# A Fourier / RG-LRU trunk on one core: the first stage emitted from a written order, its modulation vectors made as columns on TensorE, and the square roots of the last RG-LRU head split by direction

## The chip, the cores and the metric

One core of one Trainium2 chip runs the whole program. The metric is device time in microseconds (us) of one execution. Its engines are PE (TensorE matmuls; PEld is the loading of the stationary operand beside them), DVE (VectorE), ACT (ScalarE), POOL (GpSimd) and SP (SyncE), which here issues the DMAs.

## The reference, cut to what matters

128 context tokens and 1024 latent tokens, 1024 wide, pass two layers. Layer 0 mixes by a two-dimensional Fourier transform (over tokens, and over the 256 channels of each of 8 groups), layer 1 by a gated linear recurrence that runs forward and backward.

```python
def _ada(cond, w_ada, b_ada):
    m = jax.nn.silu(cond) @ w_ada + b_ada
    shift, scale, gate = jnp.split(m, 3, axis=-1)
    ...
def _layer(x, cond, p, kind, h0):
    shift, scale, gate = _ada(cond, w_ada, b_ada)
    h = _rmsnorm(x, norm_g) * (1.0 + scale) + shift
    u, z = jnp.split(h @ w_in, 2, axis=-1)
    if kind == 0:
        y = _fourier_mix(u, p["w_fmix"], p["b_fmix"])
    else:
        uc = _centred_dwconv(u, p["conv_w"], p["conv_b"])
        yf, hf = _rglru_dir(uc, ..., h0[:, 0], False)
        yb, hb = _rglru_dir(uc, ..., h0[:, 1], True)
        y = yf + yb
    out = (y * jax.nn.silu(z)) @ w_out
    return x + gate * out, state

def _rglru_dir(u, w_r, b_r, w_i, b_i, lam, h0, reverse):
    r = jax.nn.sigmoid(_blockdiag(u, w_r, b_r))
    i = jax.nn.sigmoid(_blockdiag(u, w_i, b_i))
    log_a = -LRU_C * r * jax.nn.softplus(-lam)
    bterm = jnp.sqrt(-jnp.expm1(2.0 * log_a)) * (i * u)
    ...  # h[t] = a[t] * h[t-1] + bterm[t]
```

There are two conditions, one for latent and one for context tokens, so shift, scale and gate are needed for two vectors each. Latent tokens get a position embedding first.

## The kernel before, in words

Products of fp32 operands are made of three matmuls (`mm3`, L196 to L198): each operand is split into a rounded high part (ACT copy, L185) and the rest (DVE or POOL subtraction, L186). `wload` (L190) fetches a block of weights and splits it.

**First stage (the first 109.5 us).** It folds the channel transform into `w_fmix` (`fold`, 4 blocks: 12 matmuls of 512 columns and 8 of 256 each), loads the nine token tiles x0 to x8, adds the position rows (six matmuls of one-hot rows, L315; adds at L324 on DVE and L325 on POOL) and normalises them (`xnorm`, L332 and L335, with `rsqrt_cols`, L261 to L266). A token transform follows: half differences d0 to d3 (L431) give eight PSUM tiles `psO` (12 matmuls each), quarter differences give `psT`, quarter sums `psF`. `put` (L381 on ACT, L382 on DVE) scales each result by the modulation `coef` and splits it for the next stage, whose matmuls are `pu`. The eight PSUM banks hold psO0 to psO6 and the tile `adar` at once, so psO7 starts when one of the seven has been read by `put`; `put` needs the scale.

The modulation of layer 0 is made in two ways. The scale comes from DVE: sixteen operations over 128 x 1024 (`ada_cols`, L228) multiply a block of `w_ada_0` by a row of silu values that PE has spread over all partitions (`sil`, L414). The shift comes from PE: `adar` (L445) holds 4 columns of silu stationary (`silZ`) and streams 512 columns of `w_adaN`; the row is turned into columns at the end (`adat`, L504). One row of `sil` is written to DRAM as `silD` (L463), for use in layer 1.

The order of this stage on each engine is left to the tile framework's scheduler.

**RG-LRU stage.** Here a class `Plan` (L42) lists operations with engine, cost and operands; a list scheduler orders them and they are emitted in that order (`manual_schedule`). Of each of 16 channel tiles m and two directions d, PE makes the gate products `g`, ACT makes `tr` and `ti` (L1053), `nu` (L1059) and `ga` (L1063), then `roots` (L1070) takes the square root for both directions of a tile in one operation, with a load of another activation table before and after it. DVE follows with L1074 to L1088 and the scans (L1096 forward, L1099 reverse), the sum of both (L1111) and the product with the branch `szz` (L1138), which goes to DRAM as `gD` (L1141, L1142). The list of `h` runs over 8 heads of two tiles each (14 and 15 are the last two).

**Output stage.** `out_stage` reads `gD` back by rows `gr` (L717), splits them into `gh` and `gl` (L185, L186; the first three `gl` on POOL) and makes the tiles `o` from them and `w_out` (`wo`).

Of the kernel before, what the change touches and what calls it, by code (L numbers as in the profile page):

```python
# [28 lines left out]
GAP = 3  # L29
NG = SP + GAP + S + GAP  # L30
# [12 lines left out]
class Plan:  # L43

    def __init__(self, bufs):
        self.bufs, self.ops, self.touch, self.free = bufs, [], {}, set()

    def given(self, key):
        self.free.add(key)

    def add(self, eng, cost, fn, r=(), w=(), lat=None):
        i = len(self.ops)
        if lat is None:
            lat = 0.3 if eng == "PE" else 0.12
        pre = set()
        for k in list(r) + list(w):
            pre |= {j for j, wr in self.touch.get(k, []) if wr or k in w}
        for k in list(r) + list(w):
            self.touch.setdefault(k, []).append((i, k in w))
        self.ops.append(dict(eng=eng, cost=cost, fn=fn, lat=lat, pre=pre))  # L60

    def order(self):
        ops = self.ops
        for (tag, n), us in self.touch.items():
            old = self.touch.get((tag, n - self.bufs[tag]))
            if old and us and (tag, n) not in self.free:
# [15 lines left out]

# [7 lines left out]
        assert len(topo) == n, "cycle"  # L90
# [15 lines left out]
        free, end, start = {}, {}, {}
        wait = [len(o["pre"]) for o in ops]
        ready = {i for i in range(n) if not wait[i]}
        while ready:
            best = {}  # L110
            for i in ready:
                o = ops[i]
                e = max([free.get(o["eng"], 0.0)] + [end[j] + lag(j, i) for j in o["pre"]])
                best.setdefault(o["eng"], []).append((e, i))
            pick = None
            for eng, c in best.items():
                e0 = min(c)[0]
                e, i = min((x for x in c if x[0] <= e0 + 0.15), key=lambda x: late[x[1]])
                if pick is None or e < pick[0]:
                    pick = e, i  # L120
            e, i = pick
            start[i], end[i] = e, e + ops[i]["cost"]
            free[ops[i]["eng"]] = end[i]
            ready.discard(i)
            for j in suc[i]:
                wait[j] -= 1
                if not wait[j]:
                    ready.add(j)
        self.start, self.end = start, end
# [16 lines left out]
def body(tc, nc, a):  # L146
# [76 lines left out]
    def ada_cols(layer, mts, sil, junk, tile_of=raw_tile):  # L223
        for mt in mts:
            w = tile_of(f"wada{layer}_{mt}")
# [68 lines left out]
    def xload(t):  # L294
        x = xb.tile([128, D], F32, tag="x", name=f"x{t}", bufs=8)
        SY.dma_start(x, a["x_all"][t * 128:(t + 1) * 128, :])
        return x

    posR, posC = [None] * 4, [None] * 2
    pos = xp.tile([80, 512], F32, tag="dr", name="pos", bufs=2)  # L300
    SY.dma_start(pos, a["pos"])
    hot = xb.tile([128, D], F32, tag="x", name="hot", bufs=8)

    for n, (kind, i) in enumerate((("R", 0), ("C", 0), ("R", 2), ("C", 1), ("R", 1), ("R", 3))):
        oh = hot[:, n * 128:n * 128 + 128]
        if kind == "C":
            lo, hi = 0, 64
            V.tensor_copy(oh[lo:hi].rearrange("p (r c) -> p r c", r=4),
                          ident[lo:hi, 32 * i:32 * i + 32].rearrange("p (o c) -> p o c", o=1).broadcast_to([64, 4, 32]))
        else:  # L310
            lo, hi = 64, 80
            V.tensor_copy(oh[lo:hi].rearrange("p (r c) -> p r c", r=4),
                          ident[lo:hi, 64 + 4 * i:68 + 4 * i].rearrange("p (r o) -> p r o", o=1).broadcast_to([16, 4, 32]))
        pt = ps(f"pos{kind}{i}")
        PE.matmul(pt, oh[lo:hi], pos[lo:hi], start=True, stop=True)  # L315
        if kind == "R":
            posR[i] = pt
        else:
            posC[i] = xp.tile([128, 512], F32, name=f"posC{i}")
            A.copy(posC[i], pt)  # L320

    def xpos(t, x):
        if t > 0:
            V.tensor_tensor(x[:, 0:512], x[:, 0:512], posR[(t - 1) // 2], op=ALU.add)  # L324
            PL.tensor_tensor(x[:, 512:1024], x[:, 512:1024], posC[(t - 1) % 2], op=ALU.add)  # L325

    def xnorm(ts, xs):
        for t, x in zip(ts, xs):
            ss = xb.tile([128, 1], F32, tag="ss", name=f"ss{t}", bufs=2)
            jk = xp.tile([128, D], BF16, tag="jk", name=f"jk{t}")  # L330
            xpos(t, x)
            A.activation(jk, x, AF.Square, accum_out=ss)  # L332
            rsqrt_cols(rs[:, t:t + 1], ss, xb, f"rs{t}", 1)
            if t == 0 or t > 4:
                A.activation(x, x, AF.Identity, scale=rs[:, t:t + 1])  # L335

    dh, dl = [], []

    def dft_load(j):
        n = 512 if j < 5 else 260  # L340
        r = xp.tile([128, n], F32, tag="dr", name=f"dr{j}", bufs=2)
        SY.dma_start(r, a["tdft"][j][:, 0:n])
        p = xp if j < 4 else xb
        if j < 4:
            h = p.tile([128, n], F32R, tag="dh", name=f"dh{j}", bufs=4)
            lo = p.tile([128, n], F32R, tag="dl", name=f"dl{j}", bufs=4)
        else:
            h = p.tile([128, n], F32R, name=f"dh{j}")
            lo = p.tile([128, n], F32R, name=f"dl{j}")
        A.copy(h, r)  # L350
        PL.tensor_tensor(lo, r, h.bitcast(F32), op=ALU.subtract)
        dh.append(h)
        dl.append(lo)

    def fold(gp, w):
        wh, wl = w
        wh = wh.rearrange("p (g j n) -> p g j n", g=2, j=2)
        wl = wl.rearrange("p (g j n) -> p g j n", g=2, j=2)
        gs = slice(2 * gp, 2 * gp + 2)
        for which in range(3):  # L360
            pt = ps(f"fold{gp}_{which}")
            o = pt.rearrange("p (g n) -> p g n", g=2)
            if which < 2:
                for j in range(2):
                    sl = slice(j * 128, j * 128 + 128)
                    mm3(o, fch[:, which, sl], fcl[:, which, sl], wh[:, :, j, :], wl[:, :, j, :], j == 0, j == 1)
                hl = (Ahl, Bhl)[which]
                A.copy(hl[0][:, gs, :], pt)
                V.tensor_tensor(hl[1][:, gs, :], pt, hl[0][:, gs, :].bitcast(F32), op=ALU.subtract)
            else:  # L370
                for i in range(2):
                    g = 2 * gp + i
                    for j in range(2):
                        al = alt[:, j, 8 - g:136 - g]
                        PE.matmul(o[:, i, :], al, wh[:, i, j, :], start=j == 0, stop=False)
                        PE.matmul(o[:, i, :], al, wl[:, i, j, :], start=False, stop=j == 1)
                A.copy(R[:, gs, :], pt)
                V.tensor_tensor(R[64:96, gs, :], pt[64:96, :], R[64:96, gs, :].bitcast(F32), op=ALU.subtract)

    def put(src, c, q, hi, lo):  # L380
        A.activation(hi, src, AF.Identity, scale=sc_a(0, c, q))  # L381
        V.scalar_tensor_tensor(lo, src, sc_a(0, c, q), hi.bitcast(F32), op0=ALU.mult, op1=ALU.subtract)  # L382


    silT = xb.tile([128, KD, 2], F32, name="silT")
    A.activation(silT, condT, AF.Tanh, scale=0.5)
    V.scalar_tensor_tensor(silT, silT, 1.0, condT, op0=ALU.add, op1=ALU.mult)
# [910 lines left out]
```

## Time and profile before

| | us |
|---|---|
| three runs | 1508.64, 1510.70, 1511.09 |
| median | 1510.7 |
| the profiled execution, its own time | 1507.78 |
| its span in the trace | 1506.0 |

The time of the profiled execution is taken like that of the runs; the span runs from the first to the last instruction in its trace and leaves out 1.8 us around them. All times of rows count from the span's start. Busy shares over the span: PE 97%, DVE 72%, ACT 49%, POOL 15%. An engine that is 97% busy over the whole can still idle in a stage; which stage that is has to be read from the trace by stretches.

### The profile page before, as it was taken

The page shows a single profiled execution, that of the slowest core. Times are in us where ns is not written, and L with a number is a line of the kernel's source. Part 1 is how long each engine was busy: PE and PEld are TensorE (multiplying, and loading weights), DVE is VectorE, ACT ScalarE, POOL GpSimd, SP SyncE. Part 2 cuts the span into 40 slices and gives each one's busy share as a digit, 9 for nine tenths or more (in the row PEclk, how much of TensorE's full clock was granted, in tenths as well). Part 3 has the DMA queues.
Part 4 walks back from the last instruction along what each step waited for, and adds up shares of the span by engine and source line. Part 5 has one row for each costly group of instructions (what it writes and reads, how often), then busy time and mean ns, then how long its engine had stood idle before and what let it go on. Part 6 is the DMA issues. An engine that isn't in the chain of part 4 may idle for free.

```text
span 1506.0 us, 21530 instructions
## 1 busy us (share of the span) xinstructions
PE 1462.0 (97%) x8362; PEld 1418.6 (94%) x8362; DVE 1084.6 (72%) x1588; ACT 738.6 (49%) x1110; POOL 229.1 (15%) x208
## 2 busy tenths in 40 slices
PE   8879999999999999999999999999999999899996
PEld 5458999999999999999999999999999998799996
DVE  6996445899864586747987887878787878676453
ACT  7363233322223454428756666666666666364231
POOL 6576865000001011100000000000000003000000
PEclk9979999999999999999999999999999999899998
DMA  7523667887655666621112121212121112686451
GB/s 271 184 91 108 209 200 251 307 274 238 219 192 172 198 208 221 197 86 57 48 55 72 44 72 44 72 45 72 44 63 54 58 58 84 201 284 213 147 189 48
DMA packets 81848, 212.73 MB, mean 141 GB/s; under 512 B 9345, under 2 KB 40577, under 8 KB 81617
## 3 DMA queue, kind: packets, MB, share of 16 engines
q1 hardware_dynamic: 81746, 211.36, 42.3%
q8 instruction: 65, 1.06, 0.3%
q14 instruction: 37, 0.30, 0.1%
HBM read 171.98 MB, written 39.35 MB: 140 GB/s over the span
## 4 chain that ended last, share of the span: by engine, by line
PE 48%; DVE 2%; ACT 1%; issue 1%; DMA 1%; POOL 0%; DVEq 0%; POOLq 0%; ACTq 0%
PE o L198 4%; PE o L196 4%; PE o L197 4%; PE u L198 4%; PE u L196 4%; PE u L197 4%; PE g L196 4%; PE zz L196 4%; PE zz L198 4%; PE zz L197 4%; PE g L197 4%; PE g L198 4%; DMA gr<-gD 1%; DVE nu L1099 0%; POOL gl L186 0%
## 5 line engine op out<-in xcount | busy, mean ns | idle before, releaser
L228 DVE SCALAR_TENSOR_TENSOR sil1j<-wada,sil 128x1024 bf16<-128x1024 f32 x64 | 78.0, 1219 | 10.8 <-DMA wada<-w_ada 10.6
L1016 DVE SCALAR_TENSOR_TENSOR uc<-u,tab,uc 128x1156 f32<-128x1156 f32 (+2 forms) x54 | 69.2, 1288 | 20.5 <-ACT u L999 19.1
L534 POOL TENSOR_TENSOR xr<-xr,tab 128x384 f32<-128x384 f32 (+1 forms) x24 | 23.4, 977 | 362.7 <-DMA xr<-xT 346.5
L1097 POOL COPY st<-nu 128x1 f32<-128x1 f32 x16 | 10.4, 648 | 434.0 <-DVE nu L1096 433.7
L1074 DVE SCALAR_TENSOR_TENSOR nu<-ga,nu 128x1156 f32<-128x1156 f32 x32 | 43.5, 1359 | 45.3 <-ACT tr L1070 45.3
L834 DVE SCALAR_TENSOR_TENSOR x<-o,ada,xr 128x128 f32<-128x128 f32 (+1 forms) x64 | 31.6, 513 | 58.9 <-PE o L198 56.8
L1053 ACT ACTIVATE tr<-g,gb 128x386 f32<-128x386 f32 (+1 forms) x96 | 55.4, 585 | 25.6 <-PE g L198 21.3
L185 ACT CAST gh<-gr 128x384 fp32r<-128x384 f32 x80 | 39.7, 511 | 54.9 <-DMA gr<-gD 54.7
L1002 ACT ACTIVATE uc<-u,tab 128x386 f32<-128x386 f32 (+1 forms) x48 | 32.4, 674 | 60.8 <-PE u L198 60.8
L1127 ACT ACTIVATE szz<-zz 128x386 f32<-128x386 f32 (+1 forms) x48 | 23.6, 495 | 74.7 <-PE zz L198 74.5
L186 DVE TENSOR_TENSOR gl<-gr,gh 128x384 fp32r<-128x384 f32 x77 | 40.7, 554 | 26.5 <-ACT gh L185 26.2
L625 ACT CAST uh<-pu 128x256 fp32r<-128x256 f32 (+1 forms) x32 | 12.7, 398 | 89.3 <-PE pu L198 89.1
L1053 ACT ACTIVATE ti<-g,gb 128x386 f32<-128x386 f32 (+1 forms) x96 | 52.3, 578 | 7.9 <-PE g L198 6.7
L626 DVE TENSOR_TENSOR ul<-pu,uh 128x256 fp32r<-128x256 f32 (+1 forms) x32 | 14.4, 453 | 54.9 <-ACT uh L625 54.9
L1084 DVE SCALAR_TENSOR_TENSOR ti<-ti,uc 128x1156 f32<-128x1156 f32 x32 | 42.9, 1357 | 9.6 <-ACT ti L1053 9.3
L1080 DVE SCALAR_TENSOR_TENSOR tr<-ga,tr 128x1156 f32<-128x1156 f32 x32 | 46.4, 1451 | 0.7
L741 ACT ACTIVATE sz<-z 128x384 f32<-128x384 f32 x48 | 23.1, 488 | 48.1 <-PE z L198 24.5
L1063 ACT ACTIVATE ga<-tr,sm 128x1156 f32<-128x1156 f32 x32 | 43.1, 1350 | 3.2 <-DVE nu L1099 2.0
L1059 ACT ACTIVATE nu<-tr,sp2p 128x1156 f32<-128x1156 f32 x32 | 43.4, 1356 | 1.2 <-DVE nu L1111 0.2
L1099 DVE TENSOR_TENSOR_SCAN nu<-ga,tab,ti 128x1155 f32<-128x1155 f32 x16 | 43.9, 2745 | 0.1
L1088 DVE TENSOR_TENSOR ti<-ti,tr 128x1156 f32<-128x1156 f32 x32 | 43.4, 1356 | 0.3
L1096 DVE TENSOR_TENSOR_SCAN nu<-ga,ti 128x1156 f32<-128x1156 f32 x16 | 40.9, 2555 | 0.4
(1856 smaller groups left out, 5681.0 us busy)
## 6 DMA issues: line engine op xcount, KB each, us to landing
wo<-w_out SPq DMA_DIRECT2D x96, 512.0 KB, 4.3
wada<-w_ada SPq DMA_DIRECT2D x40, 512.0 KB, 4.2
wz<-w_z SPq DMA_DIRECT2D x32, 512.0 KB, 4.0
gr<-gD SPq DMA_DIRECT2D x80, 192.0 KB, 3.6
yD<-y SPq DMA_DIRECT2D x16, 576.0 KB, 5.0
zy<-yD SPq DMA_DIRECT2D x16, 576.0 KB, 6.5
wu<-w_u SPq DMA_DIRECT2D x16, 512.0 KB, 3.8
wg<-w_gate SPq DMA_DIRECT2D x16, 512.0 KB, 3.6
```

Source lines behind the costliest of these rows:

```text
L196: PE.matmul(out, wh, xh, start=first, stop=False)
L197: PE.matmul(out, wh, xl, start=False, stop=False)
L198: PE.matmul(out, wl, xh, start=False, stop=last)
L228: V.scalar_tensor_tensor(junk, w, 0.5, sil[:, q, :], op0=ALU.mult, op1=ALU.mult, accum_out=ada[:, layer, mt, q:q + 1])
L1016: V.scalar_tensor_tensor(T["uc", m][:, lo:hi], T[ut][:, lo + t:hi + t], convw[:, m, t:t + 1], T["uc", m][:, lo:hi], op0=ALU.mult, op1=ALU.add)
L1053: A.activation(T[tg, n][:, lo:hi], T["ps", p][:, 0:hi - lo], AF.Tanh, scale=0.5, bias=gb2[:, 2 * d + mat, m:m + 1])
L1059: A.activation(T["nu", n], T["tr", n], AF.Tanh, scale=sp2[:, d, m:m + 1], bias=sp2[:, d, m:m + 1])
L1063: A.activation(T["ga", n], T["tr", n], AF.Exp, scale=sm4[:, d, m:m + 1], bias=sm4[:, d, m:m + 1])
L1074: V.scalar_tensor_tensor(T["nu", n], T["ga", n], 1.0, T["nu", n], op0=ALU.add, op1=ALU.mult)
L1080: V.scalar_tensor_tensor(T["tr", n], T["ga", n], 1.0, T["tr", n], op0=ALU.add, op1=ALU.mult)
L1088: V.tensor_tensor(ti, ti, T["tr", n], op=ALU.mult)
L1099: V.tensor_tensor_scan(nu[:, 0:L][:, ::-1], ga[:, 0:L][:, ::-1], ti[:, 0:L][:, ::-1], h0[:, 1, m:m + 1], ALU.mult, ALU.add)
```

## The change

The first stage is put in a `Plan` too, with the orders of SP and PE written out as strings (`DORD` for the DMAs; `PORD`, `QORD0`, `QORD1` for blocks of PE work), and the scheduler fills in ACT, DVE and POOL. `Plan` gets options for this: the engines whose order is fixed, pools as slots instead of rings, an operation that may run on DVE or POOL, an offset of rank (`boost`).

Scale and shift are both made as columns: each 128 x 128 block of the weights is stationary and the two columns of `silT` are the moving operand, 8 x 8 matmuls for the scale (PSUM tile `ada0`, blocks s0 to s7 of the order) and as many for the shift (`ada1`, h0 to h7). The sixteen DVE operations of layer 0, the `sil` matmuls and their copies, `adar`, `silZ` and `adat` are gone. `silD` is written from `silT` itself by two DMAs whose access runs over single elements.

```diff
+DORD = 'a p x1 c x5 t0 x2 x6 w0 t1 x8 w1 w2 t2 x3 w3 x7 s0 t3 s1 x4 s2 s3 s4 q s5 s6 s7 x0 h0 t4 t5 h1 h2 t6 h3 h4 h5 h6 h7'
+PORD = 'j0 f0 t40 f1 j1 f2 s0 f3 s1 t41 s2 u52 u42 j2 s3 j3 s4 t62 s5 t63 s6 s7 o3 o2 h0 o0 u74 o7 u64 h1 o5 o6 h2 o4 o1'
+QORD0, QORD1 = ('h3 h4', 'h5 h6 h7')
...
+    def ada_part(part, ks):
+        p = ("ps", f"ada{part}")
+        for k in ks:
+            def mms(k=k):
...
+                for m in range(KD):
+                    PE.matmul(T[p][:, 2 * m:2 * m + 2], w[:, m * 128:m * 128 + 128], silT[:, k, :],
+                              start=k == 0 and m == 0, stop=k == KD - 1 and m == KD - 1)
+            i = P.add("PE", 0.9, mms, r=[("raw" if part else "xs", f"wada{part}{k}"), ("silT", 0)], w=[p])
...
-            for k in range(4):
-                PE.matmul(pt[:, k * 128:k * 128 + 128], silT[:, 4 * i + k, q:q + 1].broadcast_to([128, 128]), ident,
-                          start=True, stop=True)
-            V.tensor_copy(sil[:, q, 512 * i:512 * i + 512], pt)
...
-                PE.matmul(pr[0:4, :], silZ[:, k, 2 - 2 * i:6 - 2 * i], w[:, 512 * i:512 * i + 512],
-                          start=k == 0 and i == 0, stop=k == KD - 1 and i == 1)
-        for k in (2 * j, 2 * j + 1):
-            ada_cols(0, [8 + k], sil, junk, lambda n: xb.tile([128, D], F32, tag="x", name=n, bufs=8))
...
-    SY.dma_start(silD, sil[0:1, :, :])
+    for q in range(2):
+        SY.dma_start(silD[0, q].rearrange("(k p) -> p k", p=128), silT[:, :, q])
```

In the list of SP the letters are a: alternating signs, p: position rows, c: channel transform, x: token tile, t: token transform, w: `w_fmix`, s and h: weights of scale and shift, q: `pdc`. POOL keeps little of the stage: most adds, the steps of the normalisation and most rests move to DVE. The first weights of the u stage are split inside the plan (`e0`, `o0`).

In the RG-LRU stage the roots of the last head are one operation for each direction, its operations get a rank offset of 30 us, and some costs of the planner change. PE's order there stays.

```diff
-            def roots():
+            def roots(ns):
                 for n in ns:
                     A.activation(T["tr", n], T["nu", n], AF.Sqrt, scale=0.25)
-            P.add("ACT", 4.9, roots, r=[("nu", n) for n in ns], w=[("tr", n) for n in ns])
+            for part in [ns] if h < 7 else [ns[0:1], ns[1:2]]:
+                P.add("ACT", 2.56 + 1.17 * len(part), lambda part=part: roots(part), r=[("nu", n) for n in part], w=[("tr", n) for n in part])
...
-                P.add("DVE", (2.56, 4.62)[d], p6, r=[("ga", n), ("ti", n)], w=[("nu", n)])
+                P.add("DVE", (2.56, 2.78)[d], p6, r=[("ga", n), ("ti", n)], w=[("nu", n)])
...
+            if h == 7:
+                P.boost = LB
```

Where the order moves, three places. The first is SP's queue at the start, before:

```order
L200 DMA tab_148<-tab 128x760
L301 DMA pos_195<-pos 80x512
L389 DMA fc_223<-fdft 128x512
L190 DMA wf0_233<-w_fmix 128x1024
L190 DMA wf1_243<-w_fmix 128x1024
L296 DMA x1_239<-x_all 128x1024
L296 DMA x5_241<-x_all 128x1024
```

and now:

```order
L239 DMA tab_148<-tab 128x760
L345 DMA dralt_212<-alt 128x272
L345 DMA drpos_219<-pos 80x512
L345 DMA x1_224<-x_all 128x1024
L721 DMA silD_117<-silT_196 128x8x1 x2
L345 DMA drfc_227<-fdft 128x512
L345 DMA x5_231<-x_all 128x1024
L345 DMA dr0_244<-tdft 128x512
L345 DMA x2_247<-x_all 128x1024
L345 DMA x6_257<-x_all 128x1024
L345 DMA wf0_273<-w_fmix 128x1024
```

The two writes of `silD` (SP waits for DVE's `silT` there) stand ahead of the channel transform and of everything else that the first fold needs, and wf0 has moved behind four token tiles.

The second is DVE at the start. Before, the rests of the first fold weights (`wf0l`, `wf1l`) come right behind the rest of the channel transform (`fcl`) and ahead of the first token tile:

```order
L396 TENSOR_TENSOR fcl_226<-fc_223,fch_225 128x512
L186 TENSOR_TENSOR wf0l_236<-wf0_233,wf0h_235 128x1024
L186 TENSOR_TENSOR wf1l_246<-wf1_243,wf1h_245 128x1024
L324 TENSOR_TENSOR x1_239<-x1_239,posR0_199 128x512
L324 TENSOR_TENSOR x5_241<-x5_241,posR2_207 128x512
```

Now the adds of x1 and x5 and their normalisation stand behind `dlfc`, and then:

```order
L465 TENSOR_TENSOR x2_247<-x2_247,posR0_229 128x512
L468 TENSOR_TENSOR x2_247<-x2_247,posC1_268 128x512
L499 SCALAR_TENSOR_TENSOR d0_282<-x1_224,rs_156,x5_231 128x1024
L465 TENSOR_TENSOR x6_257<-x6_257,posR2_240 128x512
L468 TENSOR_TENSOR x6_257<-x6_257,posC1_268 128x512
L434 TENSOR_TENSOR d1_0l_298<-d0_282,d1_0h_293 128x1024
L434 TENSOR_TENSOR wf0l_304<-wf0_273,wf0h_296 128x1024
```

The fold weights come after the first difference d0, its split and the adds of x2 and x6.

The third is ACT at tile 14, the first of the last head, before:

```order
L1063 ACTIVATE ga140_11597<-tr140_11541,sm4_6916 128x1156
L1053 ACTIVATE tr141_11607<-g14100_11581,gb2_6919 128x386
L1053 ACTIVATE tr141_11607<-g14101_11590,gb2_6919 128x384
L1053 ACTIVATE tr141_11607<-g14102_11599,gb2_6919 128x386
L1059 ACTIVATE nu141_11621<-tr141_11607,sp2p_6915 128x1156
L1063 ACTIVATE ga141_11639<-tr141_11607,sm4_6916 128x1156
L1070 ACT_TABLE_LOAD
L1070 ACTIVATE tr140_11541<-nu140_11559 128x1156
L1070 ACTIVATE tr141_11607<-nu141_11621 128x1156
L1053 ACT_TABLE_LOAD
```

and now:

```order
L1265 ACTIVATE ga140_11618<-tr140_11566,sm4_6942 128x1156
L1255 ACTIVATE tr141_11635<-g14100_11609,gb2_6945 128x386
L1272 ACT_TABLE_LOAD
L1272 ACTIVATE tr140_11566<-nu140_11590 128x1156
L1255 ACT_TABLE_LOAD
L1255 ACTIVATE tr141_11635<-g14101_11620,gb2_6945 128x384
L1255 ACTIVATE tr141_11635<-g14102_11628,gb2_6945 128x386
```

The root of direction 0 no longer waits for the gates of direction 1; the root of direction 1 follows five gate pieces, nu141, a piece of szz14 and ga141 later, with another pair of table loads.

## Rows read from the trace of the kernel before

**Rows 1.** Two lines of the page: busy time of PE, and the TensorE clock granted in 40 equal slices of the span, in tenths of full speed.

```profile
PE 1462.0 (97%) x8362; PEld 1418.6 (94%) x8362; DVE 1084.6 (72%) x1588; ACT 738.6 (49%) x1110; POOL 229.1 (15%) x208
...
PEclk9979999999999999999999999999999999899998
```

**Rows 2.** Busy time of each engine by stretches of the span; columns are the stretch, its length, PE, PEld, DVE, ACT, POOL (with instructions), the granted clock, the DMA share and GB/s.

```profile
0.00:22.30 22.30, 17.17 (x24) 6.95 (x24) 10.48 (x24) 14.37 (x25) 9.90 (x14) 1.00 0.93 353
...
71.10:94.00 22.90, 10.87 (x21) 4.69 (x21) 22.73 (x27) 9.41 (x16) 18.42 (x8) 0.63 0.37 140
94.00:109.50 15.50, 14.73 (x122) 14.38 (x120) 13.62 (x32) 12.10 (x26) 6.32 (x3) 1.00 0.34 105
...
1225.00:1272.20 47.20, 47.20 (x267) 46.89 (x265) 33.45 (x30) 35.78 (x45) 7.55 (x5) 1.00 0.19 67
1272.20:1309.00 36.80, 27.80 (x116) 24.91 (x116) 29.66 (x35) 11.79 (x21) 5.77 (x5) 0.81 0.54 171
```

**Rows 3.** What PE waited for in the first 170 us: tile and line, releaser, us in total, times, longest.

```profile
PE psO L196 <- DVE Qol L382: 7.4, 1, 7.4
PE adar L445 <- DMA wadaN<-w_adaN: 4.6, 1, 4.6
...
PE fold L375 <- DVE rs2y L264: 1.4, 1, 1.4
```

**Rows 4.** The timeline of PE in the first stage: start, us, engine, line, operation, out<-in, count and, in brackets, idle time before it. The `us` of a row overlap; the pace is the distance of the starts. Of fold block 1 the first row, and the first of block 2; of the tokens with j = 3 two rows with 15 matmuls from one to the other; the second of psO7's twelve; the first rows of psT, of psF and of the next stage.

```profile
16.22 1.22 PE L196 MATMUL fold<-wf0h,fch 128*128 128x512 f32 x2
17.24 0.63 PE L197 MATMUL fold<-wf0l,fch 128*128 128x512 f32 x1
17.66 0.63 PE L198 MATMUL fold<-wf0h,fcl 128*128 128x512 f32 x1
...
24.17 0.39 PE L196 MATMUL fold<-wf1h,fch 128*128 128x512 f32 x1
...
27.84 0.40 PE L196 MATMUL fold<-wf2h,fch 128*128 128x512 f32 x1
...
67.33 0.39 PE L198 MATMUL psO<-dh,d_3l 128*128 128x512 f32 x1
...
70.75 0.39 PE L198 MATMUL psO<-dh,d_3l 128*128 128x512 f32 x1
...
89.66 0.63 PE L197 MATMUL psO<-dl,d_0h 128*128 128x512 f32 x1
...
94.22 0.28 PE L196 MATMUL psT<-dh,d_0h 128*128 128x256 f32 x1
...
99.88 0.28 PE L196 MATMUL psF<-dh,s_0h 128*128 128x260 f32 x1
...
109.50 0.38 PE L196 MATMUL pu<-Qoh,e0h 128*128 128x256 f32 x1
```

**Rows 5.** The only fp32 matmuls of this kernel with a 128 x 128 stationary operand and two moving columns (the sums of the final normalisation): three of them, which the trace records as six, in the timeline of PE, with the matmul behind them.

```profile
524.63 0.80 PE L788 MATMUL r<-ones,ssum 128*128 128x2 f32 x6
525.30 0.42 PE L196 MATMUL o<-gh,wo0110h 128*128 128x384 f32 x1
```

**Rows 6.** Groups by line of the first 109.5 us: busy us, mean ns of one, idle time before.

```profile
L228 DVE SCALAR_TENSOR_TENSOR silj<-wada,sil 128x1024 bf16<-128x1024 f32 x16 | 30.6, 1910 | 0.3
L445 PE MATMUL adar<-wadaN,silZ 128*4 128x512 f32 x32 | 17.0, 670 | 4.6 <-DMA wadaN<-w_adaN 4.6
```

**Rows 7.** The start: timelines of SP (a DMA issue of 128 rows), ACT and DVE, in the columns of rows 4.

```profile
7.88 0.33 SPq L393 DMA_DIRECT2D altr<-alt  x1
...
3.94 0.21 ACT L386 ACTIVATE silT<-tab 128x16 f32<-128x16 f32 x1 [1.93 <-DMA tab<-tab]
...
7.82 1.04 ACT L185 CAST wf0h<-wf 128x1024 fp32r<-128x1024 f32 x1 [0.83 <-DMA wf<-w_fmix]
...
14.20 1.28 ACT L261 ACT_TABLE_LOAD   x1
...
8.90 1.22 DVE L186 TENSOR_TENSOR wf0l<-wf,wf0h 128x1024 fp32r<-128x1024 f32 x1 [1.18 <-ACT wf0h L185]
```

**Rows 8.** What PE waited for from 1240 to 1312 us and, the last row, DVE from 1225 to 1312, in the columns of rows 3.

```profile
PE o L197 <- DVE gl L186: 4.4, 3, 1.8
PE o L196 <- ACT gh L185: 2.6, 1, 2.6
...
DVE nu L1074 <- ACT tr L1070: 7.5, 2, 5.8
```

**Rows 9.** The end of the last head and the start of the output stage: timelines of ACT, DVE, SP and PE, in the columns of rows 4. The two rows of L1138 are the gated tiles 14 and 15.

```profile
1234.08 1.28 ACT L1070 ACT_TABLE_LOAD   x1
...
1236.57 1.36 DVE L1074 SCALAR_TENSOR_TENSOR nu<-ga,nu 128x1156 f32<-128x1156 f32 x1 [5.83 <-ACT tr L1070]
...
1245.07 1.35 DVE L1074 SCALAR_TENSOR_TENSOR nu<-ga,nu 128x1156 f32<-128x1156 f32 x1
...
1263.09 1.36 DVE L1138 SCALAR_TENSOR_TENSOR szz<-szz,nu 128x1155 f32<-128x1155 f32 x1
...
1299.31 1.35 DVE L1138 SCALAR_TENSOR_TENSOR szz<-szz,nu 128x1155 f32<-128x1155 f32 x1
...
1270.38 9.95 SPq L717 DMA_DIRECT2D gr<-gD  x6
...
1274.80 0.49 PE L196 MATMUL o<-gh,wo_0h 128*128 128x384 f32 x1 [2.56 <-ACT gh L185]
```

More of the change, by code (lines that the diff above doesn't have):

```diff
@@ L292, in ps, with xa @@
         return pp.tile([128, 512], F32, tag="ps", name=name)
[L294 to L297, printed above, removed]
+    P = Plan({"raw": 3, "hi": 4, "lo": 4, "xs": 4, "d": 2, "dr": 2, "dh": 4, "ps": 8}, fixed=("SP", "PE"), handles={"DVE": V, "POOL": PL})
+    T, xa_ops = {}, []
+    X = {t: ("xs" if t > 4 else "x", t) for t in range(9)}
+    def xa(i):
+        xa_ops.append(i)
+        return i
@@ L299, in body, with silu @@
+    f_raw("uL0", a["w_u0"][0][:, 0])
+    f_raw("uR0", a["w_u0"][0][:, 1])
+    silT = misc.tile([128, KD, 2], F32, name="silT")
+    def silu():
+        A.activation(silT, condT, AF.Tanh, scale=0.5)
+        V.scalar_tensor_tensor(silT, silT, 1.0, condT, op0=ALU.add, op1=ALU.mult)
+    P.add("ACT", 0.4, silu, w=[("silT", 0)])
+    hot = xp.tile([128, 768], F32, name="hot")
     posR, posC = [None] * 4, [None] * 2
-    pos = xp.tile([80, 512], F32, tag="dr", name="pos", bufs=2)
-    SY.dma_start(pos, a["pos"])
@@ L337, in body @@
[L337 to L353, printed above, removed]
@@ L359, in fold @@
+    def fold(gp):
+        ks = split_ops(("raw", f"wf{gp}"), f"wf{gp}", f"wf{gp}")
         gs = slice(2 * gp, 2 * gp + 2)
         for which in range(3):
[L361 to L372, printed above, removed]
-                    for j in range(2):
[L374 to L387, printed above, removed]
-    fc = xp.tile([128, 512], F32, tag="dr", name="fc", bufs=2).rearrange("p (w n) -> p w n", w=2)
-    SY.dma_start(fc, a["fdft"])
@@ new lines, in body, with quarter, diff, add @@
+    for key in PORD.split():
+        block(key)
+    d4 = dft_split(4)
+    def quarter(i, sub):
+        x0, x1, d = ("x", 1 + i), ("x", 3 + i), ("d", 4 + i)
+        def diff(e):
+            T[d] = xb.tile([128, D], F32, tag="d", name=f"d2_{i}", bufs=2)
+            e.tensor_tensor(T[d], T[x0], T[x1], op=ALU.subtract)
+        def add(e):
+            e.tensor_tensor(T[x0], T[x0], T[x1], op=ALU.add)
+        if sub:
+            P.add("DVE", (1.22, 2.42), diff, r=[x0, x1], w=[d])
+            return split_ops(d, f"q{i}", f"d2_{i}")
+        P.add("DVE", (1.22, 2.42), add, r=[x1], w=[x0])
+        return split_ops(x0, f"s{i}", f"s2_{i}")
```

552 lines of the change are left out of this document (358 added, 194 removed).

## The prediction

> **What bounds the kernel now.** Over the span PE is busy 97% of the time, and the granted clock dips at the left end and near the right end of the 40 slices [rows 1]. So the middle is matmul-bound at full clock, and a change to ACT, DVE or SP pays only where PE idles or runs slowly. The table of stretches shows where. From 71.1 to 94.0 us PE works 10.87 of 22.90 us at a mean granted clock of 0.63, while DVE is busy 22.73: DVE is the bound. From 1272.2 to 1309 PE works 27.80 of 36.80 us at 0.81; just before, from 1225 to 1272.2, it never idles [rows 2]. The waits name the causes. Early, psO7 waits 7.4 us for the first put (its scale comes from the sixteen DVE operations, 30.6 us in all), and adar 4.6 us for weights [rows 3, 6]. Late, `o` waits for the pieces of gD, and DVE had waited 7.5 us for the roots [rows 8]. The change touches exactly these two places, so I cost two sums.
>
> **The first stage: when does PE start, and how much has it to do?** Before, the folds start at 16.22 and the next stage at 109.50 [rows 4].
>
> The start. The six position matmuls still come first, but the fold weights now stand on ACT and DVE behind token tiles 1 and 5. Before, the table load after the first square ended at 14.20 + 1.28 = 15.5 [rows 7]; a copy of posC1 that stood ahead of it is now behind, which takes about 0.6 off. Between the load and wf0h there are then a square and a scaling of x5, a square of x2, the copy of d0 and that of wf0, five passes of about 1.04 us [rows 7], and six small operations, some 2.4 us together. That gives 22.5 for wf0h (14.9 + 5.2 + 2.4), an estimate from these rows; the rest of wf0 follows 1.22 us later. I start the folds at 22.5, **6.3 us later** than before. Bounds: 21 if ACT waits nowhere, 27 with the write of silD at its dearest (below).
>
> The work behind it, in PE's order:
> - Folds: block 1 took 27.84 - 24.17 = 3.67 us; four make 14.7. Like the first block now (0.42 us from one matmul to the next at 17.24, against 0.23 later), the first 6 us will go at half pace: +3.1 [rows 4].
> - Tokens: 15 matmuls from 67.33 to 70.75, 0.228 each; eight tiles of 12 make 21.9 [rows 4].
> - Modulation: 128 fp32 matmuls of two columns. The one like them in the trace is `r`, three in 525.30 - 524.63 = 0.67 us, 0.223 each [rows 5]; 128 take **28.5**. Lower bound: if the two records of each overlapped, 0.11 and 14.3. I take 0.223, since it is the same shape and operand type.
> - psT and psF: 14.73 busy in the stretch from 94.0 [rows 2], less 0.8 for the removed transposes of the shift row: 13.9.
>
> What goes: adar's streams (17.0 us of records that overlap, so somewhat less [rows 6]) and the waits of 7.4 and 4.6 us [rows 3]. The scale is now ready when ada0's eighth block is, ahead of psO7 and psO6 in PE's order, so their banks come free earlier. I keep 1.4 us of waiting, like that for rs2 now [rows 3]; up to 5 if the differences d2, d3 come late on DVE, whose 30.6 us of scale work [rows 6] go but which takes over adds and rests from POOL.
>
> Sum: 22.5 + 14.7 + 3.1 + 21.9 + 28.5 + 13.9 + 1.4 = **106.0**, against 109.5: a gain of 3.5. PE's work grows by more than ten microseconds; the gain is idle time, filled.
>
> **The write of silD.** SP now stands still until silT is there, about 4.4 (3.94 + 0.21 and a short DVE step), and then issues two DMAs ahead of the channel transform, x5, x2, x6 and wf0. A DMA of 128 rows holds SP 0.33 us [rows 7]; two make 0.7, which is in the sum and hidden by the position matmuls. The Trainium skill (DMA: Bandwidth & Descriptors, Rules for kernel authors) says that an access whose last dimension isn't contiguous becomes one descriptor per element, and here that is 1,024 elements in each DMA; no run shown has such a DMA. By the rows, if 1,024 elements cost like eight DMAs of 128 rows, both hold SP 16 x 0.33 = 5.3 us, 4.6 more, and all loads behind them come so much later. By that the sum would be 110.6, and the stage would be 1.1 us slower than now. I take the cheap value because the position matmuls cover a good part, and keep the other in the range.
>
> **The last head.** ACT's first root of tile 14 comes after nu141 and ga141 now; the table load stands at 1234.08 and DVE starts on it at 1236.57 after 5.83 us idle [rows 9]. With the split it follows ga140 and one gate piece directly, about 4 us earlier. The other direction can't start before its own root, and a second pair of loads (1.28 each) is in its way, so DVE's step for it stays near 1245.07 [rows 9]. Behind that the rank offset puts the head's steps next to each other: 1.36 twice, two products, two shorter ones and the scan make about 11 us, so that the gated tile 14 would be made near 1256 rather than 1263.09, and by the same count tile 15 some 10 us ahead of 1299.31.
>
> What does that give? From 1272.2 to 1309 PE does 116 matmuls; at the pace of the stretch before (47.20 / 267 = 0.177) these need 20.5 of 36.8 us, so 16.3 are lost [rows 2]. The first 2.6 go if `gr` isn't issued at 1270.38 but earlier [rows 8, 9]. The others hang on the pieces `gl`, which DVE makes between its scans (4.4 us of waiting in three [rows 8]), and on SP's queue, in which loads of `wo` and the later `gr` take turns. I take **6 of the 16.3**, between 0 (the queue hands out pieces as before) and 11 (only the clock's return and the POOL pieces remain). The two added pairs of table loads cost nothing on PE: ACT is busy 35.78 of 47.20 us there [rows 2].
>
> In the rest of the RG-LRU stage only the planner's costs move; PE's order is the same and PE is full at clock 1.00. I take 0, within 1 either way.
>
> **Sum**: -3.5 - 6 = -9.5 us. The profiled execution (1507.78, its span 1506.0) would take 1498.3; it stands 2.9 below the median of the three runs, 1510.7, against which I forecast **1501**.
>
> **Rivals.**
> *The clock falls in the bursts of two-column matmuls.* The order has five stretches of two or three such blocks in a row (s3 s4; s6 s7 h0; h1 h2; h3 h4; h5 to h7): 12 blocks of 8 x 0.223 = 1.8, 21 us. For it: PE was busy 17.17 of the first 22.3 us with matmuls of 16 and 64 rows, and the folds behind them still went at half pace [rows 2, 4], so being busy is not enough. Against it: behind the 0.67 us of `r` the pace is not reduced [rows 5], though that is short. Price: psO7 went at (94.22 - 89.66) / 11 = 0.41 instead of 0.228 [rows 4], so a fall costs 12 x 0.18 = 2.2 us; five cost 11, and half of the 21 us at half pace adds up to 10 more. 1501 + 11 to 21: **1512 to 1522, about 1517**, slower than before. It decides from 1.9 us per fall (9.5 / 5).
> *The element-wise write holds the queue*: +4.6, **1506**; it would need about three times that to be slower than now.
> *The modulation matmuls take 0.11 each*: -14.2, and PE then waits for its tokens, so some of it comes back: **1488**.
> *The split does nothing for PE*: `gr` is held by the queue and by its buffers, DVE's `gl` comes as late: +6, **1507**. For it: three of the waits are for `gl`, not for the roots [rows 8].
>
> **How the numbers follow.** Forecast 0.50 (1496 to 1506 by its own bounds), the clock 0.18, the write 0.10, cheap modulation 0.08, a split without gain 0.14. From 1489 to 1514 leaves out most of the clock's case and part of the cheap one. About 0.2% (3 us) can be told from no change. Faster by that (below 1507.7): nearly all of the forecast (0.48) and the cheap case, and most of the two cases near 1506 (0.15): 0.72. Slower (above 1513.7): most of the clock's case, 0.14. The rest, 0.14, is the same.
>
> **What would show it.** The folds start at 22 to 23 and the next stage at 105 to 107; blocks of `ada0` and `ada1` take 1.8 us each at granted clock 1.00; the waits for the put and for `wadaN` are gone; SP leaves the silD writes by 5.3. Late, DVE's idle time ahead of 1236 shrinks, `gr` is issued ahead of 1268, and PE's idle and slow time between 1272 and 1309 is 10 us instead of 16. Wrong would be: a granted clock under 1 from 40 to 100 us, SP in the writes beyond 8 us, PE idle between 25 and 100 us for more than 5 us, or a late stretch as long as before.

## The result, and the profile after

| | before | change |
|---|---|---|
| median of four runs, us | 1510.03 (1508.64 to 1511.09) | 1531.24 (1528.51 to 1532.10) |
| ratio, 95% | | 1.0138 (1.0120 to 1.0155) |
| profiled execution, its span | 1507.78, 1506.0 | 1528.51, 1526.7 |

The change is 21 us slower. The forecast was 1501, in a range from 1489 to 1514. Cut where PE starts a stage (the end of psF is the start of its last matmul), the spans of the two profiled executions differ by 20.7 us:

| stretch, us | before | change | difference | forecast |
|---|---|---|---|---|
| start to the first fold | 16.22 | 28.41 | +12.2 | +6.3 |
| folds to the end of psF | 92.1 | 94.6 | +2.5 | -9.8 |
| end of psF to the first `pu` | 1.2 | 10.3 | +9.1 | (in the row above) |
| `pu` to the branch z | 145.0 | 146.2 | +1.2 | 0 |
| branch z | 199.7 | 199.7 | 0.0 | 0 |
| output stage of layer 0 | 203.5 | 207.4 | +3.9 | 0 |
| RG-LRU stage | 614.2 | 612.3 | -1.9 | 0 |
| last product of the branch to PE's last group | 225.6 | 219.4 | -6.2 | -6 |
| from there to the end | 8.5 | 8.4 | -0.1 | 0 |

So the late half did what was forecast, and the first stage has three faults. On the page PE stays busy; the clock digits of slices 3 and 4, 7 and 9 in [rows 1], are 7 and 8:

```profile
PE 1478.5 (97%) x8546; PEld 1453.0 (95%) x8546; DVE 1073.3 (70%) x1585; ACT 740.1 (48%) x1111; POOL 168.6 (11%) x170
...
PEclk9978999999999999999999999999999999899998
```

The waits of PE in the first 200 us, in the columns of [rows 3]. The waits for the put and for `wadaN` are gone, as forecast. Two of more than 10 us stand in their place:

```profile
PE fold L235 <- ACT wf0h L430: 10.8, 1, 10.8
PE pu L235 <- DVE Qrl L586: 10.1, 1, 10.1
...
PE nyq L762 <- DVE w8h L757: 2.4, 1, 2.4
```

**The start.** The timelines of SP, ACT and PE:

```profile
4.23 1.01 SPq L721 DMA_DIRECT2D silD<-silT  x2
5.95 0.79 SPq L345 DMA_DIRECT2D drfc<-fdft  x1
6.78 0.43 SPq L345 DMA_DIRECT2D x<-x_all  x1
17.99 0.33 SPq L345 DMA_DIRECT2D dr<-tdft  x1
```

```profile
16.62 0.62 ACT L447 CAST dhfc<-drfc 128x512 fp32r<-128x512 f32 x1 [12.63 <-DMA drfc<-fdft]
...
27.32 1.04 ACT L430 CAST wf0h<-wf 128x1024 fp32r<-128x1024 f32 x1
```

```profile
28.41 0.80 PE L235 MATMUL fold<-wf0h,dhfc 128*128 128x512 f32 x1 [10.80 <-ACT wf0h L430]
```

SP leaves the two writes at 5.2, as the cheap value had it. But the channel transform, issued at 5.95, is in ACT's hands at 16.62 only, and SP, which needs its buffer again, issues nothing from 7.2 to 18.0. Each of the two writes landed 11.7 us after its issue. It is not only that SP issued nothing: the channel transform, already issued, took 10.7 us to land. The rates in forty slices of 0.5 us show the hole, of the change and then of the kernel before:

```profile
GB/s 0 0 0 103 140 365 371 406 180 221 410 215 32 6 1 0 29 49 21 37 33 57 25 33 4 20 25 53 53 49 37 119 307 287 328 8 0 16 90 328
DMA packets 3002, 2.23 MB, mean 111 GB/s; under 512 B 2178, under 2 KB 2306, under 8 KB 3002
```

```profile
GB/s 0 0 0 79 219 377 386 254 254 209 340 274 320 401 385 426 393 369 442 401 418 418 401 442 418 418 426 401 442 402 407 407 432 408 434 394 426 391 414 426
DMA packets 2284, 6.93 MB, mean 346 GB/s; under 512 B 250, under 2 KB 506, under 8 KB 2284
```

From 6 to 15 us the change moves less than 60 GB/s, and has 1,928 more packets under 512 bytes than before; the two writes have 2,048 elements. The Trainium skill (DMA: Bandwidth & Descriptors, Rules for kernel authors) says that a non-contiguous last dimension becomes one descriptor per element; the count of packets agrees, within what other small packets differ.

**The clock.** Busy time by stretches, in the columns of [rows 2], and the pace of PE in it:

```profile
60.00:90.00 30.00, 30.00 (x184) 26.73 (x184) 17.82 (x25) 11.63 (x18) 0.00 (x0) 0.94 0.54 178
90.00:110.00 20.00, 20.00 (x129) 20.00 (x128) 7.46 (x14) 5.20 (x12) 0.00 (x0) 0.69 0.41 131
```

```profile
46.81 1.84 PE L553 MATMUL ada<-silT,wada 128*128 128x2 f32 x16
48.51 0.48 PE L235 MATMUL fold<-wf3h,dhfc 128*128 128x512 f32 x1
...
61.89 3.63 PE L553 MATMUL ada<-silT,wada 128*128 128x2 f32 x32
...
65.70 0.40 PE L236 MATMUL psO<-dl,d_2h 128*128 128x512 f32 x1
65.93 0.39 PE L237 MATMUL psO<-dh,d_2l 128*128 128x512 f32 x1
...
75.53 5.55 PE L553 MATMUL ada<-silT,wada 128*128 128x2 f32 x48
...
82.37 0.63 PE L235 MATMUL psO<-dh,d_1h 128*128 128x512 f32 x1
82.80 0.63 PE L236 MATMUL psO<-dl,d_1h 128*128 128x512 f32 x1
...
105.42 7.90 PE L553 MATMUL ada<-silT,wada 128*128 128x2 f32 x48
113.17 0.57 PE L235 MATMUL psF<-dh,s_0h 128*128 128x260 f32 x1
```

A block by itself (16 records of its eight matmuls) takes 48.51 - 46.81 = 1.7 us. Behind the first two blocks in a row, s3 and s4, psO still goes at 0.23 per matmul. Behind three in a row, s6, s7 and h0, it goes at 0.43, and the last three blocks take 7.75 from start to start where s6, s7 and h0 took 5.4. In each of the last four of the order's five runs of blocks, or right behind it, the clock fell. From 90 to 110 us PE has no gap at all, and the mean granted clock is 0.69. By the records of the granted clock it stood at the lower level (1.2 GHz) for 23.9 us between 80 and 118. The Trainium skill (TensorE: Matmul & The Clock Gate, Part 1) says that the clock follows how busy PE has been recently. By the profile's busy time this stretch doesn't show it, since PE is busy 20.00 of 20.00 us in it; but the profile counts a two-column matmul as busy time like any other, so it can't tell whether PE was busy in the Trainium skill's sense.

**The wait of `pu`.** PE and, before it, DVE:

```profile
133.34 0.55 PE L235 MATMUL pu<-Qoh,e0h 128*128 128x256 f32 x1 [10.06 <-DVE Qrl L586]
```

```profile
118.75 1.23 DVE L710 TENSOR_TENSOR e<-uL,uR 128x1024 f32<-128x1024 f32 x1
120.01 1.22 DVE L713 TENSOR_TENSOR uL<-uL,uR 128x1024 f32<-128x1024 f32 x1
...
123.08 1.80 DVE L772 TENSOR_SCALAR dg<-tab,rs 128x128 f32<-128x128 f32 x1
...
130.70 2.23 DVE L695 TENSOR_TENSOR k0r<-k0r,kb 128x16 f32<-128x16 f32 x1
132.86 2.16 DVE L586 SCALAR_TENSOR_TENSOR Qrl<-psF,coef,Qrh 128x130 fp32r<-128x130 f32 x8
```

psF is done at 123. The eight PSUM banks hold its eight tiles, and `pu` needs one of them. The last reading of each tile, the context part of `Qrl` (130 columns), stands behind `e`, `uL`, `dg` and `k0r` on DVE, in the order that the list scheduler gave. The last 130-column readings start at 132.86, the first `pu` at 133.34.

**The late end.** It comes 27.1 us later than before, so the stretches are shifted by that:

```profile
1252.10:1299.30 47.20, 47.20 (x268) 46.87 (x266) 42.39 (x38) 41.51 (x51) 8.72 (x6) 1.00 0.21 73
1299.30:1336.10 36.80, 32.75 (x160) 30.77 (x161) 29.35 (x42) 18.75 (x33) 5.25 (x4) 0.86 0.74 241
```

```profile
1282.77 3.44 DVE L1341 SCALAR_TENSOR_TENSOR szz<-szz,nu 128x1155 f32<-128x1155 f32 x1
...
1311.87 1.35 DVE L1341 SCALAR_TENSOR_TENSOR szz<-szz,nu 128x1155 f32<-128x1155 f32 x1
```

Tile 14 is gated at 1282.77 - 27.06 = 1255.7 (forecast near 1256, 1263.09 before), tile 15 at 1311.87 - 27.06 = 1284.8 (1299.31 before). PE does 160 matmuls in the 36.8 us, not 116.

### The profile page after: what moved, and what is told of

It is laid out like the page before. It is cut to its first block, busy times and chain, and to the rows that moved or that the text cites. A ratio compares the mean times of both kernels' runs of the same rounds, so it can differ in the third digit from the quotient of the medians.

```text
span 1526.7 us, 21822 instructions
## 1 busy us (share of the span) xinstructions
PE 1478.5 (97%) x8546; PEld 1453.0 (95%) x8546; DVE 1073.3 (70%) x1585; ACT 740.1 (48%) x1111; POOL 168.6 (11%) x170
## 5 line engine op out<-in xcount | busy, mean ns | idle before, releaser
L267 DVE SCALAR_TENSOR_TENSOR sil1j<-wada,sil 128x1024 bf16<-128x1024 f32 x64 | 78.1, 1220 | 11.6 <-DMA wada<-w_ada 11.6
L1300 POOL COPY st<-nu 128x1 f32<-128x1 f32 x16 | 6.8, 424 | 491.3 <-DVE nu L1299 491.2
```

Of the source, the lines that this page charges most:

```text
L267: V.scalar_tensor_tensor(junk, w, 0.5, sil[:, q, :], op0=ALU.mult, op1=ALU.mult, accum_out=ada[:, layer, mt, q:q + 1])
```

## The experiments

All are measured against the kernel before on the same chip. The theory: three separate faults in the first stage, namely the element-wise write (about 8 us), the clock (11) and the PSUM banks (9), with a late half worth 6. The rivals: the folds come late by the new order on ACT; the clock falls by the slow start and not by the blocks; the wait of `pu` is an echo of the other two.

**e1, the write behind the loads.** Of the change, the two writes of `silD` behind the first stage's plan. Outside `manual_schedule` the tile framework places them, and it had put them fifth on SP's queue; inside, they stay behind the plan's loads:

```diff
     with tc.manual_schedule(...):
         P.emit()
+        for q in range(2):
+            SY.dma_start(silD[0, q].rearrange("(k p) -> p k", p=128), silT[:, :, q])
     ...
-    for q in range(2):
-        SY.dma_start(silD[0, q].rearrange("(k p) -> p k", p=128), silT[:, :, q])
```

> The changed kernel with one edit: the two element-wise writes of silD are issued behind all loads of the first stage instead of fifth on SP's queue. In the changed kernel the loads move 1 to 45 GB/s from 6 to 16 us, x1 (issued at 2.1) is used at 12.8 and fc at 16.6. Theory (the pieces of silD hold the DMA rings for some 10 us): fc is used by 11, the first fold starts at 21 to 23 instead of 28.4, the next stage starts 5 to 7 us earlier than 133.3, the whole is about 1525. Rival (SP's new load order does it, with wf0 behind four token tiles and the token transform waiting for a buffer of fc): the first fold stays at 27 or later and the time within 2 us of 1531.

Measured 1526.47, ratio 1.0108 (1.0093 to 1.0124). PE's first fold and its waits:

```profile
20.41 0.79 PE L235 MATMUL fold<-wf0h,dhfc 128*128 128x512 f32 x1 [3.51 <-ACT wf0h L430]
```

```profile
PE pu L235 <- DVE Qrl L586: 12.3, 1, 12.3
```

The folds start 8.0 us earlier, ahead of the forecast 22.5, so ACT's new order is not what held them to 28.4. But `pu` starts at 130.5, only 2.8 earlier, where 5 to 7 were expected, and the kernel gains 4.8. From the folds to the end of psF it takes 97.5 us instead of 94.6 (here the clock fell behind the first two blocks too, from 58.0 to 61.4), and the wait of `pu` grows by 2.2: `uR`, issued at 105.57, 0.4 us ahead of the write's new place, keeps DVE idle 2.9 us.

**e2, blocks one by one.** The order of PE's work such that two blocks of two-column matmuls never follow each other (h3 to h6 between the pairs of psT, h7 inside psF, tokens by threes):

```diff
-PORD = '... s3 j3 s4 t62 s5 t63 s6 s7 o3 o2 h0 o0 u74 o7 u64 h1 o5 o6 h2 o4 o1'
+PORD = '... j2 s3 u42 s4 j3 v02 s5 v32 s6 v03 s7 v33 o3 o2 h0 o0 u74 o7 h1 u64 o5 o6 h2 o4 o1'
...
-        for key in (QORD0, QORD1)[i].split():
-            block(key)
+            if c4 % 2:
+                block(QORD[i][c4 // 2])
```

> The changed kernel with PE's order alone edited: no two blocks of eight two-column matmuls stand side by side, token work of 1.4 to 2.7 us is between any two (the same matmuls in all). In the changed kernel the granted clock was at its lower level for 23.9 us between 80 and 118 us, behind the runs of two and three blocks. Theory (the clock falls because a run of several such blocks lasts 3.6 us and more, as rival one of the prediction had it): granted clock 1.00 from 60 to 110 us and the next stage 10 to 12 us earlier, about 1520. Rival (the share of two-column work counts, not its runs): the clock still falls in the same stretch and the time stays within 4 us of 1531.

Measured 1514.59, ratio 1.0031 (1.0019 to 1.0043): 16.6 us less than the change. Stretches and waits:

```profile
60.00:90.00 30.00, 30.00 (x194) 26.90 (x194) 18.20 (x27) 12.35 (x20) 0.75 (x1) 1.00 0.58 196
90.00:110.00 20.00, 20.00 (x176) 20.00 (x176) 10.76 (x24) 8.56 (x20) 0.30 (x1) 1.00 0.41 134
```

```profile
PE nyq L767 <- DVE w8h L762: 7.8, 1, 7.8
...
PE pu L235 <- ACT o0h L430: 0.8, 1, 0.8
```

The same matmuls, in another order, run at granted clock 1.00 from 60 to 110 us, and folds to psF take 83.7 us, where the forecast had 83.5. The start is still slow here (first fold at 29.5), so that rival falls. The order also took the wait of `pu`, probably since the blocks between psT and psF give DVE time, so the 16.6 us are not the clock's alone. And 5.4 came back at `nyq`: from `pu` to the branch z it takes 153.6 us instead of 146.2.

**e3, the readings of psF first.** A priority for all readings of psF in the list scheduler (`boost=BO` in both `put` of psF and in the copy to `k0r`).

> The changed kernel with one edit in the planner's ranks: the readings of psF (both puts and the zero-frequency copy) get the rank offset that the fold's readings have, so that DVE and ACT read each psF tile out in turn instead of leaving the eight context parts to the end. In the changed kernel PE stands still from 123.3 to 133.3, until DVE reads the context parts at 132.9. Theory (the first tile pu needs a PSUM bank that psF holds until its context part is read): the wait falls from 10.1 to 1 to 3 us, time about 1523. Rival (pu waits for the zero-frequency chain or for the first u weights e0): the wait stays at 8 or more and the time at 1531.

Measured 1526.24, ratio 1.0111 (1.0096 to 1.0126).

```profile
PE nyq L762 <- DVE w8h L757: 7.8, 1, 7.8
PE pu L237 <- POOL e0l L434: 1.2, 1, 1.2
```

The wait for the banks is gone (10.1 to 1.2), so it is DVE's order and no echo of the others. Of the 8.9 us, 5.4 come back at `nyq`, whose operand DVE now makes later; the kernel is 5.0 us faster than the change.

**e4, all three.** The edits of e1, e2 and e3 together.

> All three edits together: silD behind the loads, single blocks, psF read out in turn. Theory: the three losses are of different places and add, 6 + 11 + 8 = 25, so the next stage starts at about 108 instead of 133.3 and the time is about 1506, a few us below the kernel before, since the last head's gain of 6 us stays. Rival (one hides behind another, above all because DVE or the loads of the weights become the bound once PE starts earlier): a sum under 18, the next stage at 115 or later and the time above 1513.

Measured 1509.14, ratio 0.9998 (0.9988 to 1.0008). `pu` starts at 106.26, 3.2 ahead of before, where 106.0 was forecast. But the kernel as a whole is no faster than before:

```profile
106.49 0.28 PE L236 MATMUL pu<-Qol,e0h 128*128 128x256 f32 x1
109.98 0.38 PE L237 MATMUL pu<-Qoh,e0l 128*128 128x256 f32 x1 [3.21 <-POOL e0l L434]
...
131.57 0.55 PE L767 MATMUL nyq<-Qoh,w8h 128*128 128x256 f32 x1 [7.21 <-DVE w8h L762]
...
259.79 0.34 PE L235 MATMUL z<-hh,wz0h 128*128 128x384 f32 x1
```

Two matmuls after its start `pu` stands still for 3.2 us, since POOL has made `e0l` late; `nyq` then waits 7.2 (1.3 before). From `pu` to the branch z it takes 153.5 us instead of 145.0, so z starts 5.3 us later than before, not earlier. The output stage of layer 0 stays slower too, and the late half's gain only makes up for both. Single blocks are not proof against a fall of the clock either: here, and likewise in e7, it fell once behind one block, at pace 0.43 again. PE had waited 0.26 us for that block's weights, but it waited 0.29 at the same place in e2, where the clock stayed:

```profile
44.26 1.95 PE L553 MATMUL ada<-silT,wada 128*128 128x2 f32 x16 [0.26 <-DMA wada<-w_adaN]
...
46.97 0.63 PE L237 MATMUL psO<-dh,d_1l 128*128 128x512 f32 x1
47.40 0.63 PE L235 MATMUL psO<-dh,d_1h 128*128 128x512 f32 x1
```

**e5, the write alone in the kernel before.** Of the kernel before, `silD` written from `silT` by elements, where the change has it:

```diff
+    for q in range(2):
+        SY.dma_start(silD[0, q].rearrange("(k p) -> p k", p=128), silT[:, :, q])
...
-    SY.dma_start(silD, sil[0:1, :, :])
```

> The kernel before with one part of the change: silD is written by the two element-wise DMAs from silT, which the scheduler puts behind x5 on SP's queue, in place of one row of sil later. Theory (2,048 four-byte pieces take the rings for about 10 us whatever stands around them, as between 6 and 16 us in the changed kernel): under 50 GB/s are moved for 8 to 11 us of the first 20, x2 and x6 land that much later, and the next stage starts 3 to 8 us after 109.5 (the folds of block 0 and 1 have their weights already); time about 1515. Rival (the loads of the changed kernel waited for buffers and order): 1509 to 1511, first loads as before.

Measured 1517.58, ratio 1.0048 (1.0034 to 1.0062), 8.0 us slower. The rates of the first 20 us, in slices of 0.5 us:

```profile
GB/s 0 0 0 91 146 359 416 307 295 328 377 377 401 369 401 442 385 377 418 233 73 28 17 1 0 0 0 0 16 57 82 25 49 33 25 41 25 41 49 66
```

The hole is 10 us long here too, and later, behind the loads that were issued ahead of it; the two writes landed after 13.7 and 15.3 us. `pu` starts at 114.78 instead of 109.50, so 5.3 us are lost by then; another 2.1 go in the output stage of layer 0, far from the edit.

**e6, the last head alone in the kernel before.** The change's plan for the RG-LRU stage, with its new ranking and costs, `roots` split by direction and the rank offset of the last head; the first stage of before.

> The kernel before with the other half of the change alone: the planner's new ranking and costs in the RG-LRU stage, and the roots of the last head split by direction with the rank offset; first stage untouched. In the changed kernel the stretch from the last zz to the end is 6.2 us shorter than before and the RG-LRU stage 1.9. Theory (this half gains about 8 us by itself and its gain was covered by the first stage): 1501 to 1503. Rival (the late gain came from other states of the queues behind a later start): within 3 us of 1509.5.

Measured **1501.20**, ratio 0.9939 (0.9927 to 0.9950). The second stretch of [rows 2], shifted by 2.1 us:

```profile
1274.30:1311.10 36.80, 31.77 (x160) 29.35 (x159) 28.71 (x40) 17.94 (x32) 5.19 (x4) 0.91 0.72 236
```

160 matmuls instead of 116, as in the change. This half holds the whole gain and is the fastest version measured; it beats both kernels. Which of its parts gives how much (split, offset, ranking and costs) no run separates.

**e7, `nyq` behind the first group.** e4, with the Nyquist column computed later:

```diff
-        def prologue():
+        def nyquist():
...
+            if g == 1:
+                nyquist()
```

> All three edits of the run before, and one more: the nyquist matmuls (and the preparation of their weights w8 on DVE) go behind the second group of the u stage instead of the first; what they compute stays. With the three edits PE stood still for 7.2 us (124.4 to 131.6) for w8, which DVE made only after the backlog of the first stage, so 1.5 of the 4.5 us won ahead of the u stage were left. Theory (a third of the gain was given back at the next thing that DVE makes late): that wait falls under 2 us, the time is 1502 to 1505. Rival (DVE is the bound over the whole of the first two groups): a wait of 5 us or more turns up at the next pu or pa matmul, time 1508 or more.

Measured 1503.61, ratio 0.9963 (0.9950 to 0.9975). The waits of PE:

```profile
PE pa L847 <- DVE Ucat L770: 5.4, 1, 5.4
```

The wait of `nyq` is gone and 5.5 us of the kernel's time with it. A new one stands at `pa`, again for DVE, and the branch z still starts 4.8 us later than before (259.27). With the late half in it, this kernel remains 2.4 us slower than e6, which leaves the first stage as it was.

**e8, `silD` by rows, e0 on DVE.** e7, with silT turned into 16 rows of 128 by PE, one write of them, and `e`, `uL` and their rests on DVE alone:

```diff
+            PE.matmul(T["ps", "sr"][0:KD, q * 128:q * 128 + 128], silT[:, :, q], ident, start=q == 0, stop=q == 1)
...
-    P.add("DVE", (1.22, 2.42), even, r=[L, Rr], w=[e0])
+    P.add("DVE", 1.22, lambda: even(V), r=[L, Rr], w=[e0])
```

> As the kernel with the nyquist matmuls later, with silD written in 16 rows of 128 elements instead of 2,048 single ones (PE turns silT into rows by two small matmuls behind the position matmuls, ACT copies them), and the sums, differences and splits of the first u weights kept on DVE instead of POOL. Theory: the rows cost the rings next to nothing, the wait for e0 (3.2 us with the three edits, while POOL held it and DVE's small operations took 5.3 us beside it) falls under 1.5, time 1498 to 1502. Rival (silD behind the loads was hidden already and DVE is as late with e0 as POOL): within 2 us of the run without.

Measured 1510.26, ratio 1.0022 (1.0001 to 1.0044), a miss. From 95 to 125 us, and ACT's first reading of psT:

```profile
95.00:125.00 30.00, 23.71 (x139) 22.85 (x139) 16.80 (x52) 10.80 (x26) 0.00 (x0) 0.72 0.25 80
...
102.57 1.20 ACT L594 ACTIVATE Qrh<-psT,coef 128x256 fp32r<-128x256 f32 x3 [15.11 <-DMA silD<-hot]
```

The trace shows the first edit as the cause of the delay. The row tile lies in `hot`, a buffer of the first pool, and in this plan the readings of psT and psF come only when all users of that pool are done. The write from `hot` stood last on SP's list, issued at 99.55, and ACT stood still 15.1 us for it. Behind that psF waits 2.5 us and `pu` 2.8 for DVE, the clock is at 0.72, and `pu` starts at 115.96. So this run tells nothing of what rows cost in an early place, and what `e0` on DVE gives is not separated.

**e9, the scale by rows on PE.** e6, with DVE's sixteen operations replaced by streams of 512 columns like `adar`: eight stationary columns, shift and scale in one tile (and `silD` written by rows):

```diff
+                    PE.matmul(pr[0:8, :], silZ[:, k, 6 - 2 * r:14 - 2 * r], ws[part][:, 512 * i:512 * i + 512],
+                              start=k == 0 and r == 0, stop=k == KD - 1 and r == 3)
```

> The kernel before with the late half of the change (as in the run with the head split alone) and the scale of layer 0 made on PE another way: not as columns with 128 x 128 weights stationary, but as rows like the shift before, silu as 8 stationary columns over 512 streamed ones, both vectors in one PSUM tile and four transposes; the sixteen DVE operations and the sil matmuls go, silD is written as 16 rows; order left to the scheduler as before. Theory (what bounded the stage was DVE's 30.6 us of scale, and a stage in which PE streams 512 columns keeps its clock): PE gets 16 streamed matmuls (13.8 us) and loses the sil matmuls (3.5), the idle and slow time from 71 to 94 us (12 idle, 3 slow) goes, so the next stage starts 4 to 8 us ahead of 110.1 and the time is 1494 to 1498. Rival (the loads of the weights or POOL bound the stage next): within 2 us of 1501.

Measured 1501.48, ratio 0.9940 (0.9927 to 0.9954), the same as e6 and a miss: 1494 to 1498 was expected. The stretch from 71.1 to 94, in the columns of [rows 2]:

```profile
71.10:94.00 22.90, 20.41 (x64) 9.93 (x62) 5.77 (x14) 7.73 (x14) 14.68 (x8) 0.93 0.32 103
```

DVE falls from 22.73 to 5.77 us and PE rises from 10.87 to 20.41: PE's idle time has turned into PE's own work, and `pu` starts at 110.10, no earlier than before.

## Why the prediction was wrong

The forecast missed by 30 us: 5.9 at the first fold (+12.2 instead of +6.3), 21.4 from there to `pu` (+11.6 instead of -9.8) and 2.9 in all the rest.

- **The write of silD** was the first step that failed. I took 0.7 us, SP's time for two issues, and SP's own time was near it (1.01). The cost lay behind it: the transfers of 1,024 elements kept all others below 60 GB/s for some 10 us. Even the dear end (5.3) was worked out as time on SP and was too low. e1 gives 8.0 at the first fold; e5 gives 8.0 in the kernel's time, 5.3 of it by `pu`.
- **The clock at 1.00** was the second. Rival one happened: 94.6 - 83.7 (e2) = 10.9 us, at the foot of its 11 to 21. It had 0.18. Two more kernels on either side agree: with the change's order of PE that stretch takes 97.5 in e1 and in e3, with single blocks 84.9 in e4 and 85.0 in e7. The argument against it, that `r` leaves the pace as it was, rested on 0.67 us and told nothing of runs of 3.5 to 5.4 us.
- **1.4 us of waiting** was the third, up to 5 at most; the trace has 10.1 at one place. I looked at what frees the banks of psO, and not at the next stage, which needs a bank of psF. No rival had it. e3 shows it apart from the others.
- **Right** were the 0.223 us per modulation matmul (a block takes 1.7 to 1.8) and the waits for the put and `wadaN`, which are gone. That the sum without the three faults came out (106.0 forecast, 106.26 in e4) is partly luck: the folds start at 20.4, not 22.5, and the rest takes 85.9, not 83.5.
- **The last head** was right in size, and the signs that I named for its mechanism came: 6 forecast, 6.2 in the change and 8.3 in the kernel's median by e6. DVE's wait for the roots fell from 7.5 to 1.6 us and `gr` was issued at 1293.97 - 27.06 = 1266.9 instead of 1270.38.
- **That filled idle time is a gain** was wrong too. With the faults mended, `pu` starts 3.2 us earlier, and more than that is given back behind it, for `e0l` from POOL and for `nyq` and `pa` from DVE: the branch z starts 5.3 us later than before in e4 and 4.8 in e7. In e9, where other work on PE fills the idle time, nothing is won either.

Open: the output stage of layer 0 takes 203.5 us before, 207.4 in the change and 205.6 even in e5, whose edit lies far ahead of it. A wait of 1.7 us for `gh` is part of it; the rest is a slightly slower pace that I can't place. And the RG-LRU stage is 1.9 us shorter, where 0 within 1 was forecast; in e6 and e9, with the same plan for that stage, it is only 0.3 and 0.2 shorter, so this goes with the new first stage, by a way that no run shows.

## What to carry to other kernels

Ask of a DMA how many pieces it has and what is queued around it, not only how long its issue takes. Place runs of two-column matmuls one by one between dense work. Where a list scheduler orders one stage, give it the PSUM banks that the next stage waits for; and when one engine makes all operands, follow it past the wait that you remove, to the next thing that it makes late. Judge a stage by when the stages behind it are through, not by its first matmul.

## What the runs showed of the hardware

8 KB written in 2,048 pieces of four bytes took 11.7 us to land in the change and 13.7 and 15.3 us in e5. For some 10 us they held up nearly all other traffic of the core, ahead of most loads (under 60 GB/s in the change) and behind the first of them (under 100 GB/s in e5).

The granted clock fell with PE busy 20.00 of 20.00 us, under pairs and triples of fp32 blocks of two columns (0.69 from 90 to 110 us): in or right behind four of the five runs of blocks in the change, and all five in e1 and e3. The same blocks one by one, between matmuls of 256 and 512 columns, kept it at 1.00 from 60 to 110 us in e2. One by one is no guarantee: in e4 and e7 it fell once among the blocks, near 46 us, behind a single block.
